# Sums of x on another engine and in another place, blocks in reversed order, transposes spread between products

## The chip, the cores and the metric

The kernel runs on one core of a Trainium2 chip. The metric is the device time of one execution in microseconds (us), less is better. The core has a matrix engine (TensorE, PE), a vector engine (VectorE, DVE), a scalar and activation engine (ScalarE, ACT), a general engine (GpSimd, POOL) and a queue that issues most transfers (SyncE, SP). Each engine works through its own list in order; semaphores between the lists make one wait for another.

## The reference

A trunk of two layers over 512 positions of width 1024, in float32. The first is a retention layer with 4 heads (keys of 256, values of 512), the second a latent attention with 16 heads; each ends in a layer norm of `alpha * x + sublayer(x)`.

```
hproj = x @ w_in                       # q, k (4 x 256 each), v and gate (4 x 512 each)
q, k  = rope(q), rope(k) * 256**-0.5
o     = sum over m <= n of gamma_h**(n-m) * (q_n . k_m) * v_m
o     = normalised over each head's 512 columns, times silu(gate)
x     = layer_norm(alpha * x + o @ w_out)
c     = x @ w_down;  lat = rms_norm(c[:512]);  k_rope = rope(c[512:])
q_lat, gate = x @ w_in_b;  q = rms_norm(q_lat) @ w_uq
o     = causal softmax attention of 16 heads (keys and values from lat)
x     = layer_norm(alpha * x + (o * silu(gate)) @ w_out_b)
```

## The kernel before

Every factor of a product is kept as two numbers, a high part (a cast to fp32r on ACT) and a low part (the difference, on DVE). A product takes three matmuls: high by high, high by low, low by high (`mm3`, lines 92 to 96). `split` (line 98) makes both parts of a tile. Weights go through the class `Weights`: `W.get(name)` hands out the next weight and sees to it that two more are ready ahead (line 70); `issue` loads a tile of 128x1024 into one of eight staging buffers (tag `wst`), casts it, and takes the low part on DVE or, for every third weight after the eighth, on POOL (line 64).

Layer A starts with `xTs`, x transposed, in eight loads. `proj_qk(0)` multiplies it by the first head's q and k weights as the tiles arrive, into four PSUM banks, and then turns q and k by the rotary angles: six DVE operations of 512 columns and a split for each (lines 376 to 389). `x_forms` (line 329) makes four sums of quarters of x on POOL and splits them into s1 to s4, through three staging buffers. Then come the heads. `values_and_gates(h)` forms v and the gate together, by seven products instead of eight: p1 (x itself), p6 (s2), p2 (x), p5 (s1), p7 (s3), p4 (x), p3 (s4), each of 24 matmuls of 512 columns, with additions on DVE between them (lines 440 to 465). The weights of p6, p5 and p7 are differences of tiles of v's and g's weights, taken in the staging buffers (`w_vg`, lines 118 to 144): v's first tiles stay there from p1 to p5, g's tiles from p6 on, and v's second tiles are loaded for p2. `scores(h)` forms q by k, times the decay, and splits it (line 392). `inner(h)` multiplies the scores by v for the four blocks of rows; block n takes 3(n + 1) matmuls; its normalisation runs over DVE, POOL (a power of -0.5, line 250) and ACT. `transposes(h)` turns the result over by PE, and `out_proj` multiplies it by the output weights and adds it into `r`.

The order of the program around the change, for each head: values and gates (scores after p6), inner for blocks 0 to 3, the next head's q and k projections with their turning, the four transposes, the output projections. In the last head there is no next projection, and the transposes follow directly on inner; then each block's two output halves, its layer norm, and the transposes of x1. The loads of x into `r` are in the program behind the first head's values and gates; `r` holds xT until then, so they wait for the last reader of it.

The program's order isn't the order in which each engine works. A planner writes every engine's list before the run: by its own model of durations it takes, whenever an engine is free, the instruction that stands first in the program among those that are ready, where a tile's buffer has to be free too. So a later instruction can go ahead of an earlier one, and the list is then fixed.

In layer B, the latents (`lat`, line 642) and the query latents (lines 667 to 701) are formed from x1. The query latents are normalised block by block, with a sum, a scaling, a power on POOL, and two DVE products for each. Then `gate_b(0)` (line 716) forms the first gate, and the query latents are transposed (line 728).

Of the kernel before, what the change touches and what calls it, by code (L numbers as in the profile page):

```python
# [12 lines left out]
ALU = mybir.AluOpType  # L13
# [17 lines left out]

SC_AT = {3: (0, 0), 2: (1, 0), 0: (1, 384), 1: (2, 0)}


class Weights:
# [12 lines left out]
    def issue(self, between=None):  # L48


        nc = self.nc
        name, aps, n = self.todo.pop(0)
        st = aps() if callable(aps) else self.stage.tile([P, WC], F32, tag="wst", name="wst")
        pool, th, tl = self.place[name].pop(0) if self.place.get(name) else (self.parts, "whi", "wlo")
        hi = pool.tile([P, WC], F32R, tag=th, name="whi")
        lo = pool.tile([P, WC], F32R, tag=tl, name="wlo")
        for j, ap in enumerate(aps if isinstance(aps, list) else [aps]):
            sl = slice(j * n, (j + 1) * n)
            if j and between:
                between()  # L60
            if not callable(ap):
                nc.sync.dma_start(st[:, sl], ap)
            nc.scalar.copy(hi[:, sl], st[:, sl])  # L63
            eng = nc.gpsimd if self.n % 3 == 2 and self.n > EAGER else nc.vector
            eng.tensor_tensor(out=lo[:, sl], in0=st[:, sl], in1=hi.bitcast(F32)[:, sl], op=ALU.subtract)  # L65
        self.n += 1
        self.ready.append((name, hi, lo))

    def get(self, name):
        while self.todo and len(self.ready) < 1 + self.ahead:  # L70
            self.issue()
        got, hi, lo = self.ready.pop(0)
        assert got == name, (got, name)
        return hi, lo
# [3 lines left out]
def trunk_kernel(ctx, tc, a):  # L78
# [28 lines left out]
    def w_vg(h):  # L107
# [114 lines left out]
    mhalf = const.tile([P, 1], F32, tag="mhalf", name="mhalf")  # L222
    nc.gpsimd.memset(mhalf, -0.5)
    warm = const.tile([P, 1], F32, tag="warm", name="warm")
    nc.scalar.copy(warm, mhalf)
# [20 lines left out]
    def rsqrt(pool, dst, src, mul, eps):  # L246

        t = pool.tile([P, 1], F32, tag="rs_t", name="rs_t", bufs=4)
        nc.vector.tensor_scalar(t, src, float(mul), float(eps), op0=ALU.mult, op1=ALU.add)
        nc.gpsimd.tensor_tensor(out=dst, in0=t, in1=mhalf, op=ALU.pow)  # L250
# [55 lines left out]
    if True:  # L306
# [22 lines left out]
        def x_forms():  # L329
            a11, a12 = xv[:, 0:4, 0:256], xv[:, 4:8, 0:256]  # L330
            a21, a22 = xv[:, 0:4, 256:512], xv[:, 4:8, 256:512]
            f1, f2, f3 = (wst.tile([P, 4, 256], F32, tag="wst", name="xsum") for _ in range(3))
            nc.gpsimd.tensor_tensor(out=f1, in0=a21, in1=a22, op=ALU.add)
            nc.gpsimd.tensor_tensor(out=f2, in0=f1, in1=a11, op=ALU.subtract)
            split(*forms["s2"], f2)
            nc.gpsimd.tensor_tensor(out=f3, in0=a11, in1=a21, op=ALU.subtract)
            split(*forms["s3"], f3)
            split(*forms["s1"], f1)
            nc.gpsimd.tensor_tensor(out=f2, in0=a12, in1=f2, op=ALU.subtract)
            split(*forms["s4"], f2)  # L340
# [6 lines left out]
        def proj_qk(h):  # L347
            banks = {}
            if h == 0:
                for nm in ("q", "k"):  # L350
                    banks[nm] = [bank(), bank()]
                for k in range(KX):
                    if k % 2 == 0:
                        wh, wl = W.get("qk0")
                    xh, xl = xT(k)
                    parts = ((wh, xh), (wh, xl), (wl, xh))
                    sls = [slice((k % 2) * 512 + i * P, (k % 2) * 512 + (i + 1) * P) for i in range(4)]
                    four = banks["q"] + banks["k"]

                    steps = [(i, j) for j in range(3) for i in range(4)] if k == 0 else [(i, j) for i in range(4) for j in range(3)]  # L360
                    for i, j in steps:
                        l, x_ = parts[j]
                        nc.tensor.matmul(four[i], lhsT=l[:, sls[i]], rhs=x_, start=k == j == 0, stop=k == KX - 1 and j == 2)

            hi = pa.tile([P, 4, S], F32R, tag="bh", name="qkh")
            lo = pa.tile([P, 4, S], F32R, tag="bl", name="qkl")
            for w, nm in enumerate(("q", "k")):
                ps = banks.get(nm, [])
                for t in range(0 if ps else 2):
# [6 lines left out]
                rr = pa.tile([P, 1280], F32, tag=("sTh", "sTl")[w], name="rope")  # L376
                ta, tb = tmp("ropeA"), tmp("ropeB")
                nc.vector.tensor_tensor(out=ta, in0=ps[0], in1=cosA, op=ALU.mult)
                nc.vector.tensor_tensor(out=tb, in0=ps[1], in1=sinA, op=ALU.mult)
                nc.vector.tensor_tensor(out=rr[:, 0:S], in0=ta, in1=tb, op=ALU.subtract)  # L380
                tc_, td = tmp("ropeA"), tmp("ropeB")
                nc.vector.tensor_tensor(out=tc_, in0=ps[1], in1=cosA, op=ALU.mult)
                nc.vector.tensor_tensor(out=td, in0=ps[0], in1=sinA, op=ALU.mult)
                nc.vector.tensor_tensor(out=rr[:, S : 2 * S], in0=tc_, in1=td, op=ALU.add)
                split(
                    hi[:, 2 * w : 2 * w + 2, :].rearrange("p a b -> p (a b)"),
                    lo[:, 2 * w : 2 * w + 2, :].rearrange("p a b -> p (a b)"),
                    rr[:, 0 : 2 * S],
                )
            qk[h] = (hi, lo)  # L390
# [32 lines left out]
        def values_and_gates(h):  # L423
# [43 lines left out]
        def inner(h):  # L467
# [3 lines left out]
            for n in range(NT):  # L471
# [16 lines left out]
        def transposes(h):  # L488
            hi = pa.tile([P, NT, 4, P], F32R, tag="oTh", name="oTh")
            lo = pa.tile([P, NT, 4, P], F32R, tag="oTl", name="oTl")  # L490
            for n in range(NT):
# [8 lines left out]
            oT[h] = (hi, lo)  # L500
# [16 lines left out]
        proj_qk(0)  # L517
        x_forms()
        for h in range(H_A):
# [4 lines left out]
            inner(h)  # L524
            if h + 1 < H_A:
                proj_qk(h + 1)
            transposes(h)
            if h + 1 < H_A:
                for half in range(2):
                    w = [W.get(f"o{h}") for _ in range(2)]  # L530
                    for n in range(NT):
                        out_proj(h, half, n, w)
# [5 lines left out]
        x1l = keep.tile([P, KX, S], F32R, tag="xTl", name="x1l")  # L538
        w = [W.get("o3") for _ in range(4)]
        for n in range(NT):  # L540
# [93 lines left out]
    with tc.tile_pool(name="pb1", bufs=1) as p1:  # L634
# [21 lines left out]
        lat(0)  # L656
        for t, nm in ((cosB, "cosB"), (sinB, "sinB"), (mask, "mask"), (cosR, "cosR"), (sinR, "sinR")):
            nc.sync.dma_start(t, a[nm])
        x1_transposes(2)
        lat(1)  # L660
        x1_transposes(3)
        lat(2)
        transposed(latn[0], lat_h, lat_l, 0, 0, 4)
        lat(3)
        transposed(latn[1], lat_h, lat_l, 1, 0, 4)

        ps0 = [bank() for _ in range(NT)]
        for c in range(4):
            wh, wl = W.get("ql0")
            for n in range(NT):  # L670
# [4 lines left out]
        transposed(latn[2], lat_h, lat_l, 2, 0, 4)  # L675
        transposed(latn[3], lat_h, lat_l, 3, 0, 4)
# [39 lines left out]
        def gate_b(i):  # L716
            wh, wl = W.get(f"gb{i}")
# [15 lines left out]
        gate_b(0)  # L733
# [296 lines left out]
```

## Time and profile before

| | us |
|---|---|
| median of 3 runs | 958.33 |
| lowest and highest | 957.98 and 958.8 |
| the profiled execution | 958.76 |
| its span, first to last instruction | 957.0 |

| engine | busy, us | share of the span |
|---|---|---|
| PE matmul | 921.5 | 96% |
| PE weight load | 780.1 | 82% |
| DVE | 657.7 | 69% |
| ACT | 365.9 | 38% |
| POOL | 222.0 | 23% |

The mean granted clock of PE was 0.981 of 2.4 GHz. A profile gives for each instruction its start, its length, the line of the kernel, and out<-in by the program's names; L65 is line 65. A wait is the idle time of an engine ahead of an instruction, with the one that ended it. Matmuls overlap, so their pitch (start to start) says more than their length.

### The profile page before, as it was taken

Reading aid. Unit: us, or ns where it says so; the run is one execution under the profiler, and the core shown is the slowest. Engines: PE = TensorE matmul, PEld = TensorE weight load, DVE = VectorE, ACT = ScalarE, POOL = GpSimd, SP = SyncE. Lnnn points to the kernel's source line nnn. Section 1 sums busy time; section 2 is a strip of 40 time slices with the busy share of each in tenths; the row PEclk is TensorE's granted clock in tenths of the full one; section 3 lists DMA queues with packets and bytes.
Section 4 is the critical chain, followed back from the end, with each engine's and each line's share of the span. In section 5 each row is a group of like instructions: output and inputs, shape, how many; then the busy total and the mean of one; then the engine's idle time right before and its main releaser. Section 6 shows DMA issues by size and latency. Waiting matters only on the chain.

```text
span 957.0 us, 12030 instructions
## 1 busy us (share of the span) xinstructions
PE 921.5 (96%) x4553; PEld 780.1 (82%) x4553; DVE 657.7 (69%) x1107; ACT 365.9 (38%) x612; POOL 222.0 (23%) x127
## 2 busy tenths in 40 slices
PE   9579999999999999799999999999999999999996
PEld 6458888887888888688978888888888888888885
DVE  7987676957796779884176657474674747747567
ACT  6235224522362245313444443343433434334431
POOL 3163116310642163212041100101011011111104
PEclk9789999999999999899999999999999999999998
DMA  8425213620262124222223522333233322424222
GB/s 317 155 90 187 75 45 100 199 81 28 100 191 74 45 99 133 88 64 86 80 73 102 150 71 93 112 102 89 66 107 97 111 72 88 111 83 110 89 59 96
DMA packets 32650, 98.50 MB, mean 103 GB/s; under 512 B 4304, under 2 KB 4944, under 8 KB 32592
## 3 DMA queue, kind: packets, MB, share of 16 engines
q1 hardware_dynamic: 29088, 88.16, 28.3%
q10 hardware_dynamic: 3504, 9.57, 4.1%
q8 instruction: 36, 0.59, 0.3%
q14 instruction: 22, 0.18, 0.1%
HBM read 87.23 MB, written 2.10 MB: 93 GB/s over the span
## 4 chain that ended last, share of the span: by engine, by line
PE 86%; DVE 8%; issue 2%; DMA 2%; POOL 1%; ACT 1%; SPq 0%; DVEq 0%; POOLq 0%; ACTq 0%
PE ps L95 27%; PE ps L96 27%; PE ps L94 27%; DVE wlo L65 2%; PE ps L790 2%; DMA r<-in_xT 1%; PE ps L767 1%; PE ps L768 1%; DVE sTl L100 1%; DMA g<-in_ln_g 1%; PE ps L290 1%; PE ps L494 0%; DVE rope L380 0%; DVE gs L438 0%; DVE vl L100 0%
## 5 line engine op out<-in xcount | busy, mean ns | idle before, releaser
L63 ACT CAST whi<-wst 128x1024 fp32r<-128x1024 f32 (+3 forms) x183 | 176.1, 965 | 257.8 <-PE ps L96 115.2
L65 POOL TENSOR_TENSOR wlo<-wst,whi 128x1024 fp32r<-128x1024 f32 (+3 forms) x57 | 131.6, 2308 | 602.3 <-ACT whi L63 571.8
L65 DVE TENSOR_TENSOR wlo<-wst,whi 128x1024 fp32r<-128x1024 f32 (+3 forms) x126 | 157.4, 1251 | 83.2 <-ACT whi L63 82.8
L775 ACT ACTIVATE p<-ps,sm 128x512 f32<-128x512 f32 (+1 forms) x64 | 33.3, 526 | 66.3 <-DVE sm L772 66.3
L94 PE MATMUL ps<-qlt_h,whi 128*128 128x512 f32 x144 | 56.9, 395 | 0.0
L95 PE MATMUL ps<-qlt_l,whi 128*128 128x512 f32 x144 | 56.5, 392 | 0.0
L96 PE MATMUL ps<-qlt_h,wlo 128*128 128x512 f32 x144 | 56.3, 391 | 0.0
L96 PE MATMUL ps<-whi,oTl 128*128 128x512 f32 x128 | 51.0, 402 | 1.9 <-DVE oTl L100 1.9
L94 PE MATMUL ps<-whi,oTh 128*128 128x512 f32 x128 | 52.0, 406 | 0.0
L95 PE MATMUL ps<-wlo,oTh 128*128 128x512 f32 x128 | 51.3, 401 | 0.0
L94 PE MATMUL ps<-x1h,whi 128*128 128x512 f32 x128 | 50.6, 396 | 0.0
L95 PE MATMUL ps<-x1l,whi 128*128 128x512 f32 x128 | 50.0, 390 | 0.0
L96 PE MATMUL ps<-x1h,wlo 128*128 128x512 f32 x128 | 49.9, 390 | 0.0
L115 POOL TENSOR_TENSOR wst<-wst 128x1024 f32<-128x1024 f32 x16 | 44.4, 2790 | 8.2 <-DVE wlo L65 8.0
L94 PE MATMUL ps<-whi,ogh 128*128 128x512 f32 (+1 forms) x114 | 44.7, 392 | 0.0
L96 PE MATMUL ps<-whi,ogl 128*128 128x512 f32 (+1 forms) x114 | 44.1, 387 | 0.0
L95 PE MATMUL ps<-wlo,ogh 128*128 128x512 f32 (+1 forms) x114 | 44.0, 386 | 0.0
L841 DVE TENSOR_TENSOR r<-r,ps 128x512 f32<-128x512 f32 (+1 forms) x49 | 32.3, 670 | 10.3 <-PE ps L96 10.2
L94 PE MATMUL ps<-whi,xTh 128*128 128x512 f32 x96 | 37.6, 392 | 0.0
L96 PE MATMUL ps<-xTh,wlo 128*128 128x512 f32 x96 | 37.4, 389 | 0.0
L95 PE MATMUL ps<-wlo,xTh 128*128 128x512 f32 x96 | 37.3, 389 | 0.0
L94 PE MATMUL ps<-xTh,whi 128*128 128x512 f32 x96 | 37.3, 389 | 0.0
(243 smaller groups left out, 2440.6 us busy)
## 6 DMA issues: line engine op xcount, KB each, us to landing
wst<-in_w_g SPq DMA_DIRECT2D x24, 512.0 KB, 3.3
wst<-in_w_v SPq DMA_DIRECT2D x16, 512.0 KB, 3.3
wst<-in_w_ao SPq DMA_DIRECT2D x16, 512.0 KB, 3.7
wst<-in_w_gb SPq DMA_DIRECT2D x16, 512.0 KB, 3.9
qr<-uv ACTq DMA_DIRECT2D x64, 128.0 KB, 2.4
wst<-in_w_bo SPq DMA_DIRECT2D x16, 512.0 KB, 3.7
wst<-in_w_qk SPq DMA_DIRECT2D x12, 512.0 KB, 4.0
wst<-in_w_q SPq DMA_DIRECT2D x16, 384.0 KB, 3.1
```

The source lines that it names most:

```text
L63: nc.scalar.copy(hi[:, sl], st[:, sl])
L65: eng.tensor_tensor(out=lo[:, sl], in0=st[:, sl], in1=hi.bitcast(F32)[:, sl], op=ALU.subtract)
L94: nc.tensor.matmul(ps, lhsT=lh, rhs=rh, start=start, stop=False)
L95: nc.tensor.matmul(ps, lhsT=lh, rhs=rl, start=False, stop=False)
L96: nc.tensor.matmul(ps, lhsT=ll, rhs=rh, start=False, stop=stop)
L100: nc.vector.tensor_tensor(out=lo, in0=src, in1=hi.bitcast(F32), op=ALU.subtract)
L115: eng.tensor_tensor(out=out, in0=x, in1=y, op=ALU.subtract)
L290: nc.tensor.transpose(out=ps[:, k * P : (k + 1) * P], in_=src[:, k * P : (k + 1) * P], identity=ident)
L767: nc.tensor.matmul(ps, lhsT=rh[:, qs], rhs=krp[:, :n], start=False, stop=False)
L775: nc.scalar.activation(pp, ps, AF.Exp, bias=sm[:, qb, 1:2], scale=SCALE_B, accum_out=sm[:, qb, 2:3])
L790: nc.tensor.transpose(out=ps[:, do : do + P], in_=pr[i][:, so : so + P], identity=ident)
L841: nc.vector.tensor_tensor(out=dst, in0=dst, in1=ps, op=ALU.add)
```

## The change

1. The four sums of x go to DVE. f1 and f2 and the split of s2 come right after the first q and k projection (`x_forms_first`). The product p1 of the first head follows, and only then q and k are turned (`proj_qk(0, 0, ...)`, `proj_qk(0, 1, ...)`), and the other sums and splits made (`x_forms_rest`).
2. For the first head, all low parts of the weights p1 to p7, and the differences of p5 and p7, are taken on DVE instead of partly on POOL.
3. In all heads, `scores` comes after the product p2 instead of before it.
4. `inner`, the transposes, the output projections and the latents take the blocks of rows in the order 3, 2, 1, 0.
5. In heads 0 to 2 the transposes stand between the next head's q projection and its k projection.
6. In the last head the order is: inner 3, 2, 1, transposes 3, inner 0, transposes 2, and then for each block the first output half, the transposes of the block after the next, and the second half.
7. The query latents' sum, scaling and power are done for all four blocks at once, and the first gate asks for one weight ahead instead of two.

```diff
+ORD = (3, 2, 1, 0)
+        self.on_vector = {f"p{i}.0" for i in range(1, 8)}
-            eng = nc.gpsimd if self.n % 3 == 2 and self.n > EAGER else nc.vector
+            eng = nc.gpsimd if self.n % 3 == 2 and self.n > EAGER and name not in self.on_vector else nc.vector
-    def get(self, name):
-        while self.todo and len(self.ready) < 1 + self.ahead:
+    def get(self, name, ahead=None):
+        while self.todo and len(self.ready) < 1 + (self.ahead if ahead is None else ahead):
...
-            sub(s["v1", t], s["v1", t], s["g1", t], nc.gpsimd)
+            sub(s["v1", t], s["v1", t], s["g1", t], nc.gpsimd if h else nc.vector)
...
-            return sub(s["g0", t], s["g1", t], s["g0", t], nc.gpsimd)
+            return sub(s["g0", t], s["g1", t], s["g0", t], nc.gpsimd if h else nc.vector)
...
+        def x_sum(x_, y, op):
+            f = wst.tile([P, 4, 256], F32, tag="wst", name="xsum")
+            nc.vector.tensor_tensor(out=f, in0=x_, in1=y, op=op)
+            return f
+
+        def x_forms_first():
+            f1 = x_sum(a21, a22, ALU.add)
+            f2 = x_sum(f1, a11, ALU.subtract)
             split(*forms["s2"], f2)
+            return f1, f2
+
+        def x_forms_rest(f1, f2):
             split(*forms["s1"], f1)
+            split(*forms["s3"], x_sum(a11, a21, ALU.subtract))
+            nc.vector.tensor_tensor(out=f2, in0=a12, in1=f2, op=ALU.subtract)
             split(*forms["s4"], f2)
...
             ps1 = product(f"p1.{h}", block(0, 0))
             for n in range(2):
                 nc.scalar.copy(m[:, 0, n, :], ps1[n])
+            if h == 0:
+                proj_qk(0, 0, four[:2])
+                proj_qk(0, 1, four[2:])
+                x_forms_rest(*sums)
             ps6 = product(f"p6.{h}", form("s2"))
             for n in range(2):
                 plus(m[:, 1, n, :], m[:, 0, n, :], ps6[n])
+            ps2 = product(f"p2.{h}", block(4, 0))
             scores(h)
-            ps2 = product(f"p2.{h}", block(4, 0))
...
-        proj_qk(0)
-        x_forms()
-        for h in range(H_A):
+        four = first_qk()
+        sums = x_forms_first()
+        last = H_A - 1
+        for h in range(last):
             values_and_gates(h)
...
-            inner(h)
-            if h + 1 < H_A:
-                proj_qk(h + 1)
-            transposes(h)
...
+            inner(h, ORD)
+            proj_qk(h + 1, 0)
+            transposes(h, ORD)
+            proj_qk(h + 1, 1)
+            for half in range(2):
+                w = [W.get(f"o{h}") for _ in range(2)]
+                for n in ORD:
+                    out_proj(h, half, n, w)
+        values_and_gates(last)
...
+        inner(last, ORD[:3])
+        transposes(last, ORD[:1])
+        inner(last, ORD[3:])
+        transposes(last, ORD[1:2])
         w = [W.get("o3") for _ in range(4)]
-        for n in range(NT):
-            out_proj(3, 0, n, w[:2])
-            out_proj(3, 1, n, w[2:])
+        for i, n in enumerate(ORD):
+            out_proj(last, 0, n, w[:2])
+            if i + 2 < NT:
+                transposes(last, ORD[i + 2 : i + 3])
+            out_proj(last, 1, n, w[2:])
             ln_apply(keep, n, g1, b1, ln_stats(keep, n), 2)
-            if n >= 2:
-                x1_transposes(n - 2)
+            if i >= 2:
+                x1_transposes(ORD[i - 2])
...
-            nc.vector.tensor_tensor(out=ss[:, n, 3:4], in0=ss[:, n, 1:2], in1=ss[:, n, 2:3], op=ALU.add)
-            rsqrt(p1, rs[:, n, 1:2], ss[:, n, 3:4], 1.0 / QL, RMS_EPS)
             nc.scalar.copy(krt[:, n, 1, :], ps1[n][:, 256:320])
+        nc.vector.tensor_tensor(out=ss[:, :, 3], in0=ss[:, :, 1], in1=ss[:, :, 2], op=ALU.add)
+        nc.vector.tensor_scalar(ss[:, :, 3], ss[:, :, 3], 1.0 / QL, RMS_EPS, op0=ALU.mult, op1=ALU.add)
+        nc.gpsimd.tensor_tensor(out=rs[:, :, 1], in0=ss[:, :, 3], in1=mhalf, op=ALU.pow)
...
-        gate_b(0)
+        gate_b(0, 1)
```

## Rows read from the trace of the kernel before

**Rows 1.** The page, its first part: busy time, share of the span, instructions.

```profile
PE 921.5 (96%) x4553; PEld 780.1 (82%) x4553; DVE 657.7 (69%) x1107; ACT 365.9 (38%) x612; POOL 222.0 (23%) x127
```

**Rows 2.** PE's waits: who for whom, total us, times, longest us.

```profile
PE ps L95 <- DVE wlo L65: 9.0, 3, 6.3
PE ps L94 <- ACT whi L63: 7.9, 1, 7.9
PE ps L494 <- ACT gs L486: 4.9, 4, 1.7
PE ps L290 <- DVE gsb L725: 1.9, 1, 1.9
PE ps L96 <- DVE oTl L100: 1.9, 1, 1.9
```

**Rows 3.** Four stretches: length; busy PE, PEld, DVE, ACT, POOL; clock; DMA; GB/s.

```profile
32.00:74.00 42.00, 25.12 (x91) 19.47 (x90) 38.38 (x39) 13.82 (x19) 15.97 (x6) 0.76 0.42 139
216.00:224.00 8.00, 6.12 (x26) 4.68 (x25) 8.00 (x10) 3.31 (x6) 2.38 (x1) 0.79 0.19 66
385.00:398.00 13.00, 8.10 (x31) 5.91 (x31) 10.27 (x22) 7.85 (x11) 2.20 (x4) 0.74 0.24 81
485.00:492.00 7.00, 4.82 (x35) 4.08 (x35) 6.56 (x11) 4.82 (x11) 5.08 (x5) 1.00 0.37 103
```

**Rows 4.** PE's timeline, first head: start, length, line, out<-in [idle time before].

```profile
32.13 0.39 PE L95 MATMUL ps<-wlo,xTh 128*128 128x512 f32 x1
32.35 0.39 PE L96 MATMUL ps<-whi,xTl 128*128 128x512 f32 x1
40.66 1.22 PE L94 MATMUL ps<-whi,s2h 128*128 128x512 f32 x2 [7.92 <-ACT whi L63]
...
68.50 0.80 PE L95 MATMUL ps<-wlo,s1h 128*128 128x512 f32 x1 [6.34 <-DVE wlo L65]
...
76.17 0.39 PE L94 MATMUL ps<-whi,s3h 128*128 128x512 f32 x1
```

**Rows 5.** DVE's timeline, first head.

```profile
15.78 2.83 DVE L100 TENSOR_TENSOR xTl<-r,xTh 128x512 fp32r<-128x512 f32 x1
...
21.34 3.42 DVE L100 TENSOR_TENSOR s1l<-xsum,s1h 128x1024 fp32r<-128x1024 f32 x1
...
34.48 0.68 DVE L380 TENSOR_TENSOR rope<-ropeA,ropeB 128x512 f32<-128x512 f32 x1
35.08 1.22 DVE L115 TENSOR_TENSOR wst<-wst 128x1024 f32<-128x1024 f32 x1
36.22 0.68 DVE L383 TENSOR_TENSOR ropeB<-ps,sinA 128x512 f32<-128x512 f32 x1
```

**Rows 6.** POOL's timeline, the first sum of x.

```profile
15.27 2.79 POOL L333 TENSOR_TENSOR xsum<-r 128x1024 f32<-128x1024 f32 x1 [13.96 <-DMA cosA<-in_cosA]
```

**Rows 7.** SP's timeline: issues of loads, start and length.

```profile
31.54 1.62 SPq L45 DMA_DIRECT2D wst<-in_w_v  x2
33.21 1.85 SPq L523 DMA_DIRECT2D r<-in_x  x4
```

**Rows 8.** The transfers: count, KB each, median us from issue to landing.

```profile
wst<-in_w_v SPq DMA_DIRECT2D x16, 512.0 KB, 3.3
...
r<-in_x SPq DMA_DIRECT2D x4, 512.0 KB, 7.6
```

**Rows 9.** DVE's timeline, last head: low parts of the scores and of v.

```profile
350.78 2.37 DVE L100 TENSOR_TENSOR sTl<-sf,sTh 128x512 fp32r<-128x512 f32 x1
...
378.19 1.67 DVE L100 TENSOR_TENSOR vl<-v,vh 128x512 fp32r<-128x512 f32 x1 [0.69 <-ACT vh L99]
```

**Rows 10.** PE's timeline, last head: the first matmul of inner.

```profile
378.69 0.39 PE L94 MATMUL ps<-vh,sTh 128*128 128x512 f32 x1
```

**Rows 11.** DVE's timeline at the query latents' transposes.

```profile
486.97 2.61 DVE L65 TENSOR_TENSOR wlo<-wst,whi 128x768 fp32r<-128x768 f32 x2
```

**Rows 12.** PE's timeline at the query latents' transposes.

```profile
490.23 0.44 PE L290 MATMUL ps<-ident,qn 128*128 128x128 f32 x2 [1.93 <-DVE gsb L725]
```

More of the change, by code (lines that the diff above doesn't have):

```diff
@@ L327, in form @@
             return at
[L329 to L334, printed above, removed]
+        a11, a12 = xv[:, 0:4, 0:256], xv[:, 4:8, 0:256]
+        a21, a22 = xv[:, 0:4, 256:512], xv[:, 4:8, 256:512]
+        def x_sum(x_, y, op):
[5 more added lines that the diff above has]
+            f2 = x_sum(f1, a11, ALU.subtract)
             split(*forms["s2"], f2)
-            nc.gpsimd.tensor_tensor(out=f3, in0=a11, in1=a21, op=ALU.subtract)
-            split(*forms["s3"], f3)
+            return f1, f2
+        def x_forms_rest(f1, f2):
             split(*forms["s1"], f1)
-            nc.gpsimd.tensor_tensor(out=f2, in0=a12, in1=f2, op=ALU.subtract)
+            split(*forms["s3"], x_sum(a11, a21, ALU.subtract))
+            nc.vector.tensor_tensor(out=f2, in0=a12, in1=f2, op=ALU.subtract)
             split(*forms["s4"], f2)
@@ L345, in tmp, with first_qk, proj_qk @@
             return pa.tile([P, S], F32, tag="tmpA", name=name, bufs=3)
[L347 to L369, printed above, removed]
+        def first_qk():
+            four = [bank() for _ in range(4)]
+            for k in range(KX):
+                if k % 2 == 0:
+                    wh, wl = W.get("qk0")
+                xh, xl = xT(k)
+                parts = ((wh, xh), (wh, xl), (wl, xh))
+                sls = [slice((k % 2) * 512 + i * P, (k % 2) * 512 + (i + 1) * P) for i in range(4)]
+                steps = [(i, j) for j in range(3) for i in range(4)] if k == 0 else [(i, j) for i in range(4) for j in range(3)]
+                for i, j in steps:
+                    l, x_ = parts[j]
+                    nc.tensor.matmul(four[i], lhsT=l[:, sls[i]], rhs=x_, start=k == j == 0, stop=k == KX - 1 and j == 2)
+            return four
+        def proj_qk(h, w, ps=None):
+            if w == 0:
+                hi = pa.tile([P, 4, S], F32R, tag="bh", name="qkh")
+                lo = pa.tile([P, 4, S], F32R, tag="bl", name="qkl")
+                qk[h] = (hi, lo)
+            hi, lo = qk[h]
+            if ps is None:
+                ps = []
+                for t in range(2):
                     wh, wl = W.get(f"qk{h}")
@@ L375, in proj_qk @@
                         mm3(p_, (wh[:, sl], wl[:, sl]), xT(k), k == 0, k == KX - 1)
[L376 to L390, printed above, removed]
+            rr = pa.tile([P, 1280], F32, tag=("sTh", "sTl")[w], name="rope")
+            ta, tb = tmp("ropeA"), tmp("ropeB")
+            nc.vector.tensor_tensor(out=ta, in0=ps[0], in1=cosA, op=ALU.mult)
+            nc.vector.tensor_tensor(out=tb, in0=ps[1], in1=sinA, op=ALU.mult)
+            nc.vector.tensor_tensor(out=rr[:, 0:S], in0=ta, in1=tb, op=ALU.subtract)
+            tc_, td = tmp("ropeA"), tmp("ropeB")
+            nc.vector.tensor_tensor(out=tc_, in0=ps[1], in1=cosA, op=ALU.mult)
+            nc.vector.tensor_tensor(out=td, in0=ps[0], in1=sinA, op=ALU.mult)
+            nc.vector.tensor_tensor(out=rr[:, S : 2 * S], in0=tc_, in1=td, op=ALU.add)
+            split(
+                hi[:, 2 * w : 2 * w + 2, :].rearrange("p a b -> p (a b)"),
+                lo[:, 2 * w : 2 * w + 2, :].rearrange("p a b -> p (a b)"),
+                rr[:, 0 : 2 * S],
+            )
         def scores(h):
@@ L465, in values_and_gates, with inner @@
                 gated(n, plus(c[:, n, :], c[:, n, :], ps3[n]))
-        def inner(h):
+        def inner(h, ns):
             sh, sl_, at = sT[h]
@@ L470, in inner @@
             o = gs[h]
-            for n in range(NT):
+            for n in ns:
                 ps = bank()
@@ L486, in inner, with transposes @@
                 nc.scalar.activation(o[:, n, :], o[:, n, :], AF.Copy, scale=rs)
[L488 to L491, printed above, removed]
+        def transposes(h, ns):
+            if ns[0] == ORD[0]:
+                oT[h] = tuple(pa.tile([P, NT, 4, P], F32R, tag="oT" + e, name="oT" + e) for e in "hl")
+            hi, lo = oT[h]
+            for n in ns:
                 ps = bank()
@@ L499, in transposes @@
                 )
-            oT[h] = (hi, lo)
         def out_proj(h, half, n, w):
@@ L669, in trunk_kernel @@
             wh, wl = W.get("ql0")
-            for n in range(NT):
+            for n in ORD:
                 for j in range(2):
@@ L714, in trunk_kernel, with gate_b @@
         gsb = {}
-        def gate_b(i):
-            wh, wl = W.get(f"gb{i}")
+        def gate_b(i, ahead=None):
+            wh, wl = W.get(f"gb{i}", ahead)
             ps = bank()
```

32 lines of the change are left out of this document (13 added, 19 removed).

## The prediction

> **What bounds the kernel now.** I read the page's first part first: TensorE (PE) is busy 96% of the span [rows 1], so a gain can only come from the few places where it waits or runs slow. The waits of PE come next [rows 2]: five groups, 25.6 us together, nearly all of it behind VectorE (DVE) or ScalarE (ACT) work that prepares an operand. The table of stretches puts them in place [rows 3]: 32 to 74 us (first head; PE busy 25.1 of 42, granted clock 0.76), 216 to 224 (0.79), 385 to 398 (last head; 0.74) and 485 to 492. After most waits PE also runs at 1.2 instead of 2.4 GHz for some microseconds, so each wait costs more than its length.
>
> The first head is the largest. The product with x's first block ends at 32.35 + 0.23 = 32.6, and the first matmul of p7 starts at 76.17 [rows 4]. Between them lie p6, p2 and p5 (72 matmuls at the pitch 32.35 - 32.13 = 0.227 us, 16.3 us) and the scores (24 narrower ones, 320 columns on the mean; I take 3.9 us). That is 20.2 us of work in 43.6: 23.4 lost. What is late there is DVE: busy 38.4 of the 42 us [rows 3]. Part of its time is not work: a 512-wide difference of 0.69 takes 2.83 while GpSimd (POOL) runs its sum of x (2.79), and a 1024-wide one takes 3.42 [rows 5, 6]. Undisturbed, DVE starts its operations 0.60 us apart (512 wide, 34.48 to 35.08) and 1.14 apart (1024 wide, 35.08 to 36.22) [rows 5].
>
> **The first head's part of the change.** It takes GpSimd out of this stretch: four sums, and for weights p1 to p7 four differences and four low parts, go to DVE, at 1.14 each. Two of the low parts and two differences fall behind the point considered, so DVE gains 8 operations, 9.1 us up to the end of p5. In return it loses the lengthenings: about 2.2 each on the two 512-wide and two of the 1024-wide operations near 16 to 31 (8.7 in all), and about as much again near 52 to 68. DVE's list up to p5's end gets some 8 us shorter, and its order changes. Step by step, from 16.5, when the last low part of x is due:
>
> Before the turning: one 0.68 low part, two of p1, f1, f2, s2's low part (5 x 1.14) and p6's four differences and two low parts (6 x 1.14): 13.2 us, so 29.7. Casts on ACT and the weights' loads sit beside it; I allow 1.3 for two turning operations slipping in, 31.0. PE arrives at 32.6, so the 7.9 us wait and the 2 us one after it go. PE does p6 until 38.0. The turning then takes 12 x 0.60 + 2 x 1.14 = 9.5 us of DVE; with the above DVE is through at 39.3, so the scores wait 1.3 us and run until 43.1.
>
> Then the rest of the sums, 5 x 1.14: until 45.0. Two additions (1.2) and p5's first low part bring 47.4: PE waits 4.3 us, with some 2.4 of slow clock after it (between the 8 x 0.21 = 1.7 and 13 x 0.26 = 3.4 of two other waits [rows 3]). Of p2 the weight tiles have no free staging buffer until s3 and s4 are split (43.9 and 45.0): f1 and f2 now live past the turning, and eight buffers are two for v, four for g and these. Before, the same two loads left at 31.5, ahead of the four loads of x into r [rows 7]. Now these four come in front on the one queue, ready when the last sum has read r (42.7); such a load lands after 7.6 us against 3.3 for a tile of v [rows 8], so I let v's land 4.3 later: 51.5, its low part 53.8. If p5 goes first it fills PE from 47.4 to 55.2 (5.4 + 2.4), p2 follows without a wait and ends at 60.7. From 45.0 to p7's second low part DVE has ten 1024-wide operations (low parts of p5, p2 and p7, differences of p5 and p7; 11.4) and the narrower ones of the additions, the scores and v (8.1), 19.5 in all, so until 64.5, about 1 us later than p7 wants it, and PE is close behind it for two more products: 2.5 us. Gain: 76.2 - 60.7 - 2.5 = **13.0**. Bounds: 8 (p2 ahead of p5, below) and 17 (neither wait loses the clock, DVE just ahead).
>
> DVE's pitch is below its operations' durations (0.60 against 0.68, 1.14 against 1.22 [rows 5]). The Trainium skill (VectorE: DVE Perf Modes, The DRAIN you can't avoid) lets the next operation in only when the pipe has run empty, unless it is one that is not held. Were these held, some 45 operations at 0.08 would make this list 3.6 us longer, the gain 9.4 and the total 939.9. The rows show them overlapping, so the sum goes by the pitch.
>
> **Transposes between the q and the k projection** (heads 0 to 2). Before, the low parts of the transposed output stand on DVE behind k's turning; at 218 us that cost a wait of 1.9 [rows 2] and 8 x 0.21 = 1.7 of clock [rows 3]. Now k's projection, 48 matmuls or 10.9 us, covers them, and k's turning lies under the output projection. Gain **3.6**, bounds 0 and 3.6; the other two heads show no such wait. What is late next there is nothing visible: the transposes' own input has q's 10.9 us as cover.
>
> **Last head.** The four groups of transposes wait 4.9 us in all [rows 2], and the clock costs 13 x 0.26 = 3.4 more [rows 3]: 8.3. Now two of the four groups stand behind a half of the output projection (12 matmuls, 2.7 us) and are covered; of the other two waits, 2.4, block 0 of inner (3 matmuls) covers 0.7, leaving 1.8, with 1.7 of clock. The longest block first also needs the last block of v after 9 matmuls: inner starts at 378.69, so at 380.7, and that low part ended at 378.19 + 1.67 = 379.9 [rows 9, 10]. The margin is 0.9 us; the scores' DVE work, moved behind p2, may eat it: 0.3. Gain **4.5**, bounds 1 and 7.9.
>
> **Query latents.** Two low parts (2.6 us) precede on DVE the gate's operation whose bank PE waits for, 1.9 us [rows 2, 11, 12]. The gate now asks for one weight less ahead, so I take one of the two out: **1.3**. The root for all four blocks at once must wait for the last one, so the bounds are -1.5 and 2.2 (all the idle time there [rows 3]).
>
> **At nothing.** Reversed row order in the output projection, the latents and their transposes: as many matmuls, and the block finished first is used first. Scores behind p2 in heads 1 to 3: PE's work is the same, and inner, the only reader, comes four products of 5.4 us later. The loads of x into r: first read after the whole head.
>
> **Sum.** The profiled execution took 958.76 (span 957.0 and 1.76 around it), 0.43 above the median of 958.33. 13.0 + 3.6 + 4.5 + 1.3 = 22.4, so 936.4 on its scale and **936** on the median's.
>
> **Rivals.** *p2 is held in front of p5.* The order on PE is written before the run by the planner's own clock. If it expects v's tiles early, PE stands from 43.1 until the cast at 52.6 instead of 47.4: 5 us more, **941**. For it: in the trace p2 comes before p5. Against: the buffers are short in the planner's account too. The Trainium skill (PSUM — Partial Sum Buffer, Engine vs sequencer instructions) has matmuls start in program order, so no ready p5 would step in; by that rule the time is this 941, and the trace agrees so far that the 6.3 us wait was filled by nothing [rows 2].
>
> *The moves do less than they say.* If the planner puts the rest of the sums in front of the turning, where DVE has a moment, the scores come 5.7 later, less some 2 for v's earlier loads and plus 2 of clock: **942**. For it: before, the sums of x did run ahead of the turning though they stand behind it in the program [rows 5]. Against: p6's weights now stand between.
>
> *Inner waits for v in every head.* With the scores behind p2, their four low parts (the first took 2.37 under POOL's work [rows 9]; I put all four at 5.5) and four multiplications (1.9 by their widths), 7.4 us in all, fall into the stretch in which v must be ready. If all of it lands ahead of v's last low part, inner, longest block first, starts 7.4 less a margin of 0.9 to 2.5 late, 5 us, plus 1.7 of clock, in each of four heads: 27, so 958.8 - 22.4 + 27 = **963**, slower. It decides when DVE is more than 5 us behind at v's last block. For it: the margin of 0.9. Against: the planner gives v's parts rank over later weights, and DVE has idle time in the earlier heads.
>
> **Chances.** Forecast 0.60; p2 held 0.18; moves do less 0.12; inner waits 0.06; something unnamed 0.04. The low end takes all bounds on the good side, 17 + 3.6 + 7.9 + 2.2 = 30.7, to 927; the high end goes past the two middle rivals together, 947, to 949. A difference under 0.2% (1.9 us) is what can't be told from no change: faster 0.90, same 0.04, slower 0.06.
>
> **What would show it.** Right: no POOL work before the second head; no wait of PE at 32.6, a short one ahead of the scores, one of about 4 us near 43 to 48, p7 near 61 to 64; no wait for oTl between the second and third heads; near the last transposes two waits, not four. Wrong: a wait of PE on a cast of p2's weights, or on vl at the start of inner, in more than one head; DVE with idle time in the first head while PE waits for a load.

## The result and the profile after

The changed kernel took **942.81 us** (median of 4 runs, 942.06 to 943.94), against 958.15 for the kernel before on the same chip: ratio 0.9842, 95% interval 0.9825 to 0.9859. That is 15.3 us less, where 22.4 were forecast. The profiled execution took 942.06 with a span of 940.3; its mean granted clock is 0.991 against 0.981.

The page of the changed kernel, first part (answers to [rows 1]):

```profile
PE 914.9 (97%) x4553; PEld 776.0 (83%) x4553; DVE 643.4 (68%) x1113; ACT 365.8 (39%) x612; POOL 187.5 (20%) x112
```

PE executes as many matmuls as before. What it waits for (answers to [rows 2]):

```profile
PE ps L97 <- ACT whi L66: 8.5, 3, 7.5
PE ps L510 <- ACT gs L501: 2.9, 1, 2.9
PE ps L293 <- DVE gsb L749: 1.5, 1, 1.5
...
PE ps L98 <- POOL wlo L68: 1.0, 1, 1.0
PE ps L98 <- DVE wlo L68: 1.0, 1, 1.0
PE ps L99 <- DVE oTl L103: 0.7, 1, 0.7
```

Where the time came from is read by the start of the same PE stage in both traces:

| stage begins | before | after | gained so far |
|---|---|---|---|
| p7 of head 0 | 76.17 | 64.19 | 12.0 |
| inner of head 0 | 92.49 | 81.97 | 10.5 |
| p1 of head 1 | 144.80 | 134.06 | 10.7 |
| p1 of head 2 | 242.59 | 228.03 | 14.6 |
| p4 of head 3 | 367.81 | 353.03 | 14.8 |
| inner of head 3 | 378.69 | 365.21 | 13.5 |
| first product of x1 | 418.96 | 403.00 | 16.0 |
| query latents' transposes | 485.75 | 469.79 | 16.0 |
| the product behind them | 491.31 | 474.88 | 16.4 |
| end of the span | 957.0 | 940.3 | 16.7 |

So the first head gave 10.5, the transposes between q and k 3.8, the last head lost 1.3 and then gained 2.5, the query latents gave 0.5. The four places of [rows 3] where they now lie (the stretches taken for the second and the last are longer); columns as there, clock after POOL:

```profile
32.00:74.00 42.00, 32.45 (x137) 25.50 (x136) 38.48 (x49) 19.98 (x25) 0.00 (x0) 0.92 0.53 171
196.00:210.00 14.00, 14.00 (x64) 11.58 (x63) 10.91 (x13) 3.76 (x5) 2.39 (x1) 1.00 0.23 76
...
370.00:383.00 13.00, 9.34 (x40) 7.27 (x39) 11.87 (x23) 5.50 (x8) 3.55 (x5) 0.87 0.04 9
468.00:477.00 9.00, 7.29 (x46) 6.13 (x45) 9.00 (x17) 5.06 (x11) 2.79 (x3) 1.00 0.31 105
```

POOL is gone from the first head, PE is busy 32.5 of the 42 us instead of 25.1, DVE still 38.5. What PE still waits for there stands in four timelines (start, length, engine, line, out<-in, idle time before). PE, the one long wait:

```profile
45.83 0.80 PE L97 MATMUL ps<-whi,xTh 128*128 128x512 f32 x1 [7.53 <-ACT whi L66]
```

DVE, from s1's low part on (the turning begins at 25.42):

```profile
19.49 1.22 DVE L103 TENSOR_TENSOR s1l<-xsum,s1h 128x1024 fp32r<-128x1024 f32 x1
...
35.38 1.22 DVE L337 TENSOR_TENSOR xsum<-r 128x1024 f32<-128x1024 f32 x1
36.52 0.68 DVE L391 TENSOR_TENSOR ropeB<-ps,sinA 128x512 f32<-128x512 f32 x1
...
40.05 1.21 DVE L103 TENSOR_TENSOR s3l<-xsum,s3h 128x1024 fp32r<-128x1024 f32 x1
...
41.78 1.22 DVE L349 TENSOR_TENSOR xsum<-r,xsum 128x1024 f32<-128x1024 f32 x1
...
43.52 1.22 DVE L103 TENSOR_TENSOR qkl<-rope,qkh 128x1024 fp32r<-128x1024 f32 x1
44.65 1.22 DVE L103 TENSOR_TENSOR s4l<-xsum,s4h 128x1024 fp32r<-128x1024 f32 x1
...
51.92 1.22 DVE L68 TENSOR_TENSOR wlo<-wst,whi 128x1024 fp32r<-128x1024 f32 x1 [3.15 <-ACT whi L66]
```

SP's issues of the two weight tiles of p2, what each of the two waited for (SP's waits from 30 to 60 us), and ACT's casts of them:

```profile
41.29 0.33 SPq L48 DMA_DIRECT2D wst<-in_w_v  x1
43.03 0.80 SPq L539 DMA_DIRECT2D r<-in_x  x2
45.93 0.33 SPq L48 DMA_DIRECT2D wst<-in_w_v  x1
```

```profile
SPq L48 <- DVE s3l L103: 3.8, 1, 3.8
...
SPq L48 <- DVE s4l L103: 2.0, 1, 2.0
```

```profile
44.73 1.04 ACT L66 CAST whi<-wst 128x1024 fp32r<-128x1024 f32 x1 [0.66 <-DMA wst<-in_w_v]
50.84 2.00 ACT L66 CAST whi<-wst 128x1024 fp32r<-128x1024 f32 x2 [5.06 <-DMA wst<-in_w_v]
```

The reader sees: p6 ends at 38.3, and PE stands until a cast of p2's first tile, whose load could leave only when s3's low part had freed a staging buffer (40.05 + 1.21 = 41.26; issue at 41.29). The second tile stands behind two loads of x, and leaves when s4's low part has freed the next buffer (44.65 + 1.22 = 45.87; issue at 45.93). Three operations of the other sums stand between those of the turning, and s1's low part already ahead of it, so k is ready with its low part at 44.74, not at 39.3; DVE later idles 3.15 us for p2's second tile.

### The profile page after: what moved, and what is told of

Its sections match the earlier page's. It is cut to its first block, busy times and chain, and to the rows that moved or that the text cites. A ratio compares the mean times of both kernels' runs of the same rounds, so it can differ in the third digit from the quotient of the medians.

```text
span 940.3 us, 12010 instructions
## 1 busy us (share of the span) xinstructions
PE 914.9 (97%) x4553; PEld 776.0 (83%) x4553; DVE 643.4 (68%) x1113; ACT 365.8 (39%) x612; POOL 187.5 (20%) x112
## 4 chain that ended last, share of the span: by engine, by line
PE 87%; DVE 7%; issue 4%; POOL 1%; ACT 1%; DMA 1%; DVEq 0%; POOLq 0%; ACTq 0%; SPq 0%
PE ps L98 26%; PE ps L99 26%; PE ps L97 26%; PE ps L369 2%; PE ps L814 2%; PE ps L791 1%; PE ps L792 1%; DVE wlo L68 1%; PE ps L510 1%; DVE wst L118 1%; PE ps L293 1%; DMA wst<-in_w_v 1%; DVE vl L103 0%; ACT whi L66 0%; PE ps L234 0%
## 5 line engine op out<-in xcount | busy, mean ns | idle before, releaser
L68 POOL TENSOR_TENSOR wlo<-wst,whi 128x1024 fp32r<-128x1024 f32 (+3 forms) x53 | 121.6, 2294 | 641.5 <-ACT whi L66 602.9
L68 DVE TENSOR_TENSOR wlo<-wst,whi 128x1024 fp32r<-128x1024 f32 (+3 forms) x130 | 161.0, 1242 | 97.6 <-ACT whi L66 97.0
L865 DVE TENSOR_TENSOR r<-r,ps 128x512 f32<-128x512 f32 (+1 forms) x49 | 32.3, 669 | 10.5 <-PE ps L99 10.4
L98 PE MATMUL ps<-wlo,xTh 128*128 128x512 f32 x96 | 38.3, 399 | 1.0 <-POOL wlo L68 1.0
L99 PE MATMUL ps<-whi,xTl 128*128 128x512 f32 x96 | 37.9, 395 | 0.0
```

Of the source, the lines that this page charges most:

```text
L98: nc.tensor.matmul(ps, lhsT=lh, rhs=rl, start=False, stop=False)
L99: nc.tensor.matmul(ps, lhsT=ll, rhs=rh, start=False, stop=stop)
L865: nc.vector.tensor_tensor(out=dst, in0=dst, in1=ps, op=ALU.add)
```

## The experiments

Each kernel is an edit of the changed one (two of them of "sums aside"). "Inner" is the start of the first head's inner blocks, from PE's timeline; 81.97 in the changed kernel, 92.49 before. Ratios are to the kernel before, run beside each.

| edit | median, us | ratio, 95% interval | inner | span |
|---|---|---|---|---|
| (the change) | 942.81 | 0.9825 to 0.9859 | 81.97 | 940.3 |
| sums aside | 937.98 | 0.9778 to 0.9805 | 77.56 | 935.6 |
| sums on POOL | 942.81 | 0.9824 to 0.9852 | 82.06 | 940.5 |
| weights on POOL | 943.29 | 0.9834 to 0.9861 | 83.27 | 941.2 |
| old place | 941.71 | 0.9818 to 0.985 | 82.04 | 940.2 |
| scores first | 939.43 | 0.9788 to 0.9815 | 79.57 | 937.7 |
| both on POOL | 947.98 | 0.9875 to 0.9906 | 86.24 | 945.9 |
| all three old | 950.70 | 0.991 to 0.9941 | 88.14 | 947.3 |
| last together | 947.44 | 0.9875 to 0.9902 | 81.14 | 943.9 |
| last on vector | 937.40 | 0.9776 to 0.9807 | 77.61 | 935.6 |
| transposes last | 946.50 | 0.9873 to 0.9902 | 81.99 | 944.5 |
| forward | 943.86 | 0.9843 to 0.9869 | 82.20 | 941.5 |
| turn apart | 937.00 | 0.9767 to 0.9793 | 77.77 | 935.9 |

### The first head: single moves undone

**Sums aside** writes the first two sums into a tile that is idle until the gates, so that p2's loads find free staging buffers:

```
+ xs = pa.tile([P, 2, 4, 256], F32, tag="gs", name="xs")
- f1 = x_sum(a21, a22, ALU.add)
- f2 = x_sum(f1, a11, ALU.subtract)
+ f1 = x_sum(a21, a22, ALU.add, xs[:, 0])
+ f2 = x_sum(f1, a11, ALU.subtract, xs[:, 1])
```

> The changed kernel with f1 and f2 kept in the gate's tile, which is idle then, so that two staging buffers are free and the second tiles of v can be loaded some 20 us earlier. Theory A (the 7.5 us wait of TensorE at 38.3 us is the load of v's tiles, late for want of a buffer): the wait goes, p7 starts about 6 to 8 us earlier, total 935 to 937. Theory B (VectorE's list is the bound: the turning, the sums and p2's low parts take until about 44 us wherever the tiles are): the wait stays at 5 us or more, only the second small wait at 51 us and VectorE's 3.2 us of idle time at 49 us go, total 939 to 942.

Inner starts 4.4 us earlier and the time falls by 4.8. The wait at 38 us is shorter but not gone; PE's timeline names another releaser, k's turned high part:

```profile
44.37 0.79 PE L97 MATMUL ps<-qkh 128*128 128x512 f32 x1 [5.73 <-ACT qkh L102]
```

The later waits of the first head are gone. So holding the two sums in staging buffers cost the change 4.4 us, and behind that stands the late turning.

**Sums on POOL**, **weights on POOL** and **old place** undo one move each:

```
  # sums on POOL: x_sum and the last sum
- nc.vector.tensor_tensor(...)
+ nc.gpsimd.tensor_tensor(...)
  # weights on POOL
- self.on_vector = {f"p{i}.0" for i in range(1, 8)}
+ self.on_vector = set()
- nc.gpsimd if h else nc.vector      # p5, p7
+ nc.gpsimd
  # old place: ahead of p1
- sums = x_forms_first()
+ proj_qk(0, 0, four[:2]); proj_qk(0, 1, four[2:])
+ x_forms_rest(*x_forms_first())
```

> The changed kernel with its four sums of x on GpSimd again, in their new places. If the engine matters (GpSimd's operation blocks VectorE's two-operand operations for its length, about 2.2 us each, against 1.14 us saved on VectorE): 4 x 1.1 us and a later s2, total 946 to 949. If only the place of the sums matters: 942 to 944.

> The changed kernel with the first head's differences of p5 and p7 and every third low part on GpSimd again. Theory lock: eight operations of 2.4 us on GpSimd each lengthen VectorE's work by up to 2 us, against 9.1 us taken off VectorE: p7 starts 3 to 7 us later, total 946 to 950. Theory relief (VectorE is the bound and gains by each operation taken off it): total 936 to 940.

> The changed kernel with turning and all sums, on VectorE, ahead of the product p1 again, as the program had them before. If the new place matters: p6 waits at 32.6 us until turning and sums are through (some 8 us, as before the change), and the wait at 38 us shrinks by as much of it as VectorE has done by then; p7 starts 2 to 6 us later, total 945 to 949. If the planner runs ahead anyway and only the engine matters: 942 to 944.

All three stand within 1.1 us of the changed kernel. Their waits of PE show why: with the sums on POOL the waits sit in p6 and, 4.1 us long, on p2's low part; with the weights on POOL the 7.5 us wait stays; in the old place one wait of 10.2 us stands ahead of p6 and nearly nothing follows. One line of each kernel's waits, in that order:

```profile
PE ps L98 <- DVE wlo L68: 5.3, 2, 4.1
```

```profile
PE ps L97 <- ACT whi L66: 7.5, 1, 7.5
```

```profile
PE ps L97 <- ACT whi L66: 10.2, 1, 10.2
```

No single one of the three moves is worth more than the 1.3 us by which inner is later with the weights on POOL, while the other two stand: it shifts the place at which PE stands still.

### The first head: moves undone together

**Both on POOL** joins the edits of sums on POOL and weights on POOL, **all three old** adds that of old place.

> The changed kernel with two of its moves undone together: the four sums of x and the first head's block differences and low parts go back to POOL, the places and the order stay as changed. Theory A (one of the two moves is enough, because both take away the same thing, VectorE's lengthening beside POOL): with both undone VectorE's instructions of the first head lengthen again, inner blocks of head 0 start at 87 to 92, 948 to 953. Theory B (the time hangs on the total that VectorE has to do, and POOL takes a share of it): 942 to 944, as with either alone.

> The changed kernel with three of the first head's moves undone together: the sums of x and the first head's differences and low parts on POOL, and the turning and all sums ahead of p1. Of the first head's part only the scores behind p2 are left (in all heads). Theory A (the first head's 10.5 us come from taking POOL's work out of VectorE's way, and any one of the moves back costs nothing only because another takes its place): inner blocks of head 0 start at 90 to 93, as before the change, 950 to 954. Theory B (with both on POOL the place doesn't matter, as it didn't with both on VectorE): as with both on POOL in the new place, 947 to 949, inner blocks at 86 to 88.

The first came out just under theory A's span (947.98; inner 86.24): two moves undone cost 5.2 us where either alone cost 0.5 at most. By the start of inner 4.3 of that lies in the first head; 1.6 arose at the query latents, which the edit doesn't touch (last section). The second lies between its theories: the median (950.70) fits A, but its runs go from 948.54 to 952.61, and the profiled one, at 949.12, fits neither; its inner (88.14) lies just outside B's span and well short of A's 90 to 93. DVE and POOL of the kernel with both on POOL:

```profile
40.33 0.68 DVE L395 TENSOR_TENSOR ropeB<-ps,sinA 128x512 f32<-128x512 f32 x1
40.93 0.68 DVE L390 TENSOR_TENSOR ropeA<-ps,cosA 128x512 f32<-128x512 f32 x1
41.53 1.69 DVE L396 TENSOR_TENSOR rope<-ropeA,ropeB 128x512 f32<-128x512 f32 x1
43.15 3.42 DVE L103 TENSOR_TENSOR s3l<-xsum,s3h 128x1024 fp32r<-128x1024 f32 x1
...
57.26 3.36 DVE L103 TENSOR_TENSOR qkl<-rope,qkh 128x1024 fp32r<-128x1024 f32 x1
```

```profile
40.12 2.55 POOL L68 TENSOR_TENSOR wlo<-wst,whi 128x1024 fp32r<-128x1024 f32 x1 [8.86 <-ACT whi L66]
42.75 2.73 POOL L118 TENSOR_TENSOR wst<-wst 128x1024 f32<-128x1024 f32 x1
```

The lengthening of [rows 5, 6] is back: 3.4 us for work of 1.2. Beside the same POOL operation at 40.12, DVE's products that read PSUM keep their 0.68, and the sum of two SBUF tiles behind them takes 1.69, until 0.55 us after POOL's end (43.22 against 42.67). The Trainium skill (SBUF — State Buffer, SBUF: two separate sides) has the port pair that the two engines share go to one instruction at a time, a DVE operation contending, among other cases, when both its inputs lie in SBUF and POOL's operation reads SBUF; these rows agree.

The steps don't add up to a fixed worth each. From 92.49, scores behind p2 with the rest old gives 88.14; the new place 86.24; the weights to DVE 82.06; the sums to DVE 81.97. In the other order, sums first, they read 86.24, 83.27, 81.97.

### Scores, and what bounds the first head now

**Scores first** swaps two lines back, in all heads:

```
- ps2 = product(f"p2.{h}", block(4, 0))
  scores(h)
+ ps2 = product(f"p2.{h}", block(4, 0))
```

> The changed kernel with one edit: in every head the scores stand ahead of product p2 again, as in the kernel before; everything else as changed. Theory A (the first head's list of VectorE is the bound, whatever PE's order): the 7.5 us wait for p2's weights moves to the scores, the inner blocks of head 0 start at 82 (+-1) as in the changed kernel, 942 to 944. Theory B (scores behind p2 carry the first head's gain, since PE then has 12.8 us of p2 to do while VectorE turns q and k): the first head's waits return, inner blocks of head 0 from 86 to 92, 948 to 953. A side guess: if the 1.0 us wait for a low part on POOL in the last head came from moving the scores, it is gone here and the time is 1 to 2 lower than either says.

Neither theory: it is faster than the change, 939.43, and inner starts at 79.57. PE's wait at 38 is 4.69 long, until k's high part at 43.60, instead of 7.53 until p2's cast. The side guess held: p4 of the last head starts without a wait (its 1.0 us wait on POOL is not among this kernel's waits), which is 1.3 us. So the move that brought 4.35 us in the old arrangement (92.49 to 88.14, if nothing else of the change reaches that stretch; no run undoes it there) costs 2.4 in the new one and 1.3 in the last head. The span is only 2.6 shorter, since the profiled execution lost 1.6 more at the query latents (last section).

**Turn apart** takes sums aside and scores first and gives the turning more temporary tiles:

```
- ta, tb = tmp("ropeA"), tmp("ropeB")
+ ta, tb = (c[:, 1, :], c[:, 2, :]) if c is not None and w else (tmp("ropeA"), tmp("ropeB"))
- tc_, td = tmp("ropeA"), tmp("ropeB")
+ tc_, td = tmp("ropeA"), c[:, 0, :] if c is not None and w == 0 else tmp("ropeB")
```

> Three edits on the changed kernel: the first two sums in tiles of their own (as in sums aside, 937.98), the scores ahead of p2 (as in scores first, 939.43), and more temporary tiles for the first head's turning, so that in VectorE's list only one instruction of the other sums stands between the turning's operations instead of three (one sum and two low parts move behind k's turning). Theory A (what is left in the first head is the wait for the turned k, which the planner put late by slotting the sums in): that wait ends 2 to 2.5 earlier, near 42 instead of 44.4, nothing new takes its place, and the 1.0 us wait for a low part on POOL in the last head goes as it did with scores first: 933 to 935. Theory B (the total of VectorE's list up to p5 sets the end, whatever its order): the wait moves to p2, p5 or p7, and only the last head's part is gained: 936 to 938.

PE's wait:

```profile
42.94 0.80 PE L97 MATMUL ps<-qkh 128*128 128x512 f32 x1 [4.62 <-ACT qkh L102]
```

It ends 1.4 us earlier than in sums aside, yet inner starts at 77.77 against 77.56. So theory A's gain in the first head did not come, though no new wait of its size appeared: summed over PE's matmuls, the time beyond their usual pitch is 3.3 us after this wait against 2.6 there, and 0.5 more in p7. The granted clock was 0.50 (1.2 of 2.4 GHz) from the end of the wait until about 49.6 in both kernels, so that the earlier end bought more time at the lower level. Turn apart, then sums aside, columns as above:

```profile
43.00:49.50 6.50, 6.46 (x20) 5.60 (x21) 6.50 (x8) 4.09 (x5) 0.00 (x0) 0.50 0.68 215
```

```profile
44.40:49.60 5.20, 5.20 (x12) 4.10 (x13) 5.20 (x6) 0.00 (x0) 0.00 (x0) 0.50 0.00 0
```

The time, 937.0, is theory B's, but the profiled execution lost 1.6 us more at the query latents than that of sums aside (last section); the start of inner says more here than the time. DVE's share of 32 to 62 us, in the changed kernel, in sums aside and in turn apart:

```profile
32.00:62.00 30.00, 21.78 (x93) 17.32 (x92) 26.70 (x36) 12.64 (x17) 0.00 (x0) 0.89 0.53 175
```

```profile
32.00:62.00 30.00, 24.27 (x104) 19.95 (x103) 29.47 (x39) 12.20 (x18) 0.00 (x0) 0.89 0.42 140
```

```profile
32.00:62.00 30.00, 25.34 (x105) 20.99 (x105) 30.00 (x40) 12.73 (x17) 0.00 (x0) 0.89 0.39 123
```

26.7, 29.5 and 30.0 of 30: the changed kernel still left DVE idle there, the other two hardly do. That DVE's total is what is left agrees with this, but it was not shown by taking work away from it. At 937.0 this is the lowest median of the study (0.9767 to 0.9793 of the kernel before); sums aside, one edit only, and last on vector can't be told from it.

### Transposes, last head, order of the blocks

**Transposes last** puts the transposes behind the next head's k projection again:

```
  proj_qk(h + 1, 0)
- transposes(h, ORD)
  proj_qk(h + 1, 1)
+ transposes(h, ORD)
```

> The changed kernel, only that in heads 0 to 2 the transposes stand behind the next head's k projection again. Theory A (k's projection covers the low parts of the transposed output, which otherwise queue on VectorE behind k's turning): a wait for oTl of about 1.9 returns near 205 (head 1 to 2), with 1.7 of slow clock, the span grows by 3 to 4, 945.5 to 947. Theory B (VectorE's load near there changed with the rest, so the wait doesn't come back): 942 to 943.5.

The wait came back where it was expected, and the time is 946.50. One line of its waits, and the clock behind the wait:

```profile
PE ps L99 <- DVE oTl L103: 1.9, 1, 1.9
```

```profile
206.00:214.00 8.00, 6.11 (x31) 4.77 (x29) 8.00 (x10) 2.81 (x5) 2.28 (x1) 1.00 0.20 66
```

But the clock stayed at 1.00, where [rows 3] had 0.79 behind the same wait. By the starts of p1 of head 2 (230.47 against 228.03, and head 1 already 0.24 late) only 2.2 us were lost in place. 1.6 of the rest arose at the query latents, which the edit doesn't touch (last section). So the time fell into theory A's span partly by luck: the wait is as theory A has it, its price in clock is not.

**Last together** gathers inner, transposes and outputs of the last head, still last block first; **forward** keeps them spread, first block first:

```
  # last together
- inner(last, ORD[:3]); transposes(last, ORD[:1])
- inner(last, ORD[3:]); transposes(last, ORD[1:2])
+ inner(last, ORD); transposes(last, ORD)
  # forward
- ORD = (3, 2, 1, 0)
+ ORD = (0, 1, 2, 3)
```

> The changed kernel, only that in the last head all four inner blocks stand together, then all transposes, then the outputs (still last block to first). Theory A (inner blocks and transposes put between other products hide the eviction and the gating): the waits for the gating return, 2.5 us or more over the changed kernel's single wait of 2.94, 945 to 947. Theory B (the loss of the last head is the delay of VectorE and ACT beside POOL's low parts, and PE's order only moves it): 942 to 943.5.

> The changed kernel, only with the blocks in forward order (0, 1, 2, 3) everywhere; transposes and outputs still put between. Theory A (reversed order is worth nothing by itself: the first gated block is late in either order, since it is late through VectorE's gating of the gate): one wait ahead of the first transposes of 3 or so, 941 to 944. Theory B (with the longest block first, the 15 matmuls of the next two cover part of the chain behind it; in forward order the shortest block comes first and the wait falls on later blocks too): two or more waits, 944.5 to 946.

Together costs 4.6 us by the medians (947.44; the profiled execution took 945.70): four waits again, 6.5 us in all. From the start of the last head's inner to the first product of x1 it takes 42.05 us against 37.79. Forward has one wait, of 4.66 us and not 3 or so, and 943.86, inside theory A's span: about 1 us from the change, less than can be told apart.

**Last on vector** moves three low parts from POOL to DVE, on top of sums aside:

```
- self.on_vector = {f"p{i}.0" for i in range(1, 8)}
+ self.on_vector = {f"p{i}.0" for i in range(1, 8)} | {"p4.3", "p3.3", "o3"}
```

> The kernel with its first two sums in tiles of their own (the experiment sums aside, 937.98), and in the last head the low parts that POOL computes (of p4, p3 and the output weights) go to VectorE. Theory A (POOL's low parts beside the gating are what the last head still loses: a 1.0 us wait for the low part itself, and most of the 2.94 us wait for the first gated block, whose instruction took 2.45 instead of about 1.2): both go, 934 to 936. Theory B (VectorE is full there, the low parts only move the delay): 937 to 940.

937.40, as theory B has it. In the changed kernel the gating of the last head's second half took 2.45 us beside POOL's low part:

```profile
369.44 2.45 DVE L449 SCALAR_TENSOR_TENSOR gs<-th,c 128x512 f32<-128x512 f32 x1 [0.78 <-ACT th L448]
```

```profile
368.96 2.39 POOL L68 TENSOR_TENSOR wlo<-wst,whi 128x1024 fp32r<-128x1024 f32 x1 [2.89 <-ACT whi L66]
```

With that low part on DVE the gating takes 0.68 but waits behind it:

```profile
365.32 1.23 DVE L68 TENSOR_TENSOR wlo<-wst,whi 128x1024 fp32r<-128x1024 f32 x1 [0.25 <-ACT whi L66]
366.46 0.68 DVE L452 SCALAR_TENSOR_TENSOR gs<-th,c 128x512 f32<-128x512 f32 x1
```

The next operation starts at 367.06 against 367.42 in sums aside: 0.4 us for a lengthening of 1.8. The 1.0 us wait on POOL's low part is gone too, but a wait of 0.8 us for v's low part at the start of inner is new, and the first product of x1 starts at 398.16 against 398.19: the three moves together are worth nothing that these runs can show.

## Why the prediction held, and which of its steps failed

The time fell inside the range, 6.8 us above the forecast, and the four places of gain are the four that were named. It lies nearest to the second middle rival's 942, and inside the range because that was drawn past both middle rivals; of the sum, only the transposes' term came out near its size. By its terms:

**First head, 13.0 forecast, 10.5 measured.** p6 without a wait is right (it starts at 32.70, right behind p1), and so is the absence of POOL. The step that failed is "the turning then takes 9.5 us of DVE ... DVE is through at 39.3 ... then the rest of the sums". The planner put f3, s3's low part and the last sum between the turning's operations, so k's parts were done at 44.74. "If p5 goes first" failed with it: the list has p2 ahead of p5, the first rival's order, and the scores behind p2. The load of x ahead of p2's weights was right for one tile of two. Up to the start of p7 the forecast had 76.2 - 60.7 = 15.5, of which 12.0 arrived; of the 2.5 to be lost behind that, 1.5 was, with a wait of 1.0 us for a low part inside p7, at granted clock 1.00 (64 to 72 us). Both middle rivals were priced at 941 and 942 on these two steps, and both steps happened, though not at their prices: the cast of p2's first tile ended at 45.77, of the second at 51.88, where the rival had 52.6. One of the signs named for being wrong came too, in small: DVE idles 3.15 us for a load while PE waits 0.7 for it.

**Transposes, 3.6 forecast, 3.8 measured**, and the mechanism is confirmed by undoing it. Some 1.6 of it was clock and not wait, and in the undone kernel the clock did not fall, which is why only 2.2 us came back.

**Last head, 4.5 forecast, 1.2 measured.** This is the term that was most mis-sized. That only two waits would be left was nearly right (2.9 and 0.7), and the spreading itself is worth 4.3 us in the changed kernel (42.05 - 37.79 above). But the first gated block was late for another reason than the order: the gating stands beside or behind a low part, whichever engine takes it, and in the changed kernel ACT's cast of that weight (367.85 to 368.88) stands ahead of the activation that the gating reads; no run takes the low part out of there, so how much of the wait is due to it stays open. And "scores behind p2 in heads 1 to 3" was costed at nothing; it made PE wait 1.0 us for a low part on POOL and cost 1.3:

```profile
354.43 0.50 PE L98 MATMUL ps<-wlo,xTh 128*128 128x512 f32 x1 [1.01 <-POOL wlo L68]
```

**Query latents, 1.3 forecast, 0.5 measured.** One of two low parts was to leave DVE ahead of the gate; both are still there, only shorter (1.81 for both against 2.61 in [rows 11]; POOL's work now ends before they start, at 470.86). No run undoes this part alone; the reading rests on these rows:

```profile
471.33 1.81 DVE L68 TENSOR_TENSOR wlo<-wst,whi 128x768 fp32r<-128x768 f32 x2
473.07 0.67 DVE L749 SCALAR_TENSOR_TENSOR gsb<-thb,ps 128x512 f32<-128x512 f32 x1
```

The terms measured add to 10.5 + 3.8 + 1.2 + 0.5 = 16.0; the span fell by 16.7, the rest in three steps of less than 0.3 between and behind them. The third rival (inner waiting for v in every head) did not occur: no wait on vl stands among the changed kernel's waits.

That the sum went by the pitch of DVE's operations and not by their lengths was right: in the changed list they still start 1.14 apart (35.38 to 36.52 above) and 0.60 (36.52 to 37.12).

## What to carry to other kernels

Where one engine feeds the bottleneck, the worth of moving its work need not be a sum of parts, as it wasn't here: undo pairs, not only single edits, before calling a move idle or useful. Where a planner sets the order, code that stands later in the program can fill gaps in a critical chain and make it late; what holds a buffer from there on is a cost of its own (two sums in staging buffers cost 4.4 us here).

## What was not expected of the hardware

The clock behind a wait is not a fixed price. The same wait of 1.9 us for oTl had granted clock 0.79 behind it in the kernel before and 1.00 in transposes last, a difference of 1.6 us of PE's time beyond its pitch (3.8 against 2.2). At the query latents, whose code the edits of the study don't touch (but for forward's order of blocks), a wait of 1.5 us is followed by a clock of 1.00 in the changed kernel and of 0.79 in transposes last (474 to 482 us, in that order):

```profile
474.00:482.00 8.00, 7.75 (x37) 6.32 (x37) 5.19 (x12) 2.68 (x5) 2.39 (x1) 1.00 0.25 98
```

```profile
474.00:482.00 8.00, 6.29 (x27) 4.89 (x26) 7.00 (x13) 3.53 (x10) 0.00 (x0) 0.79 0.34 117
```

From the first of the query latents' transposes to the first product of them it takes 7.92 us in the one and 9.52 in the other. Scores first, both on POOL and turn apart show the 9.5 as well, the other experiments the 7.9, so up to 1.6 us of any comparison above is of this kind. What decides it was not tested.
